# Sharing the last multiplication of a decoder step between VectorE and GpSimd

## The chip, the cores and the metric

The kernel runs on one core of a Trainium2 chip. The metric is device time in microseconds of one execution; the number compared is the median over several executions. Engine names: TensorE (PE) multiplies matrices into PSUM, VectorE (DVE) and ScalarE (ACT) work on PSUM and SBUF, GpSimd (POOL) is used here on SBUF only, SyncE (SP) issues DMAs. Stores of the result are issued from the queues of SyncE and ScalarE.

## What is computed

One decoding step of a hybrid layer for 256 prompt tokens and 32 sample tokens (288 columns, `NT`): RMSNorm, one wide input projection into a gated convolution, sparse attention and memory attention, one output projection, a residual addition and a last RMSNorm. Only that last norm is touched:

```python
def rms_norm(x, g):
    xf = x.astype(jnp.float32)
    y = xf * lax.rsqrt(jnp.mean(xf * xf, axis=-1, keepdims=True) + NORM_EPS)
    return (y * g.astype(jnp.float32)).astype(x.dtype)
...
    return x + mixed @ w_out, kv_new, win_state, conv_new
...
    y_prompt = rms_norm(xp, final_g)
    y_sample = rms_norm(xs, final_g)
```

## The kernel before

The model width of 2048 lies as 16 planes of 128 partitions, tokens along the free axis, so the result `ysum` is a tile of 128 x 16 x 288 floats in SBUF, and `o_y` in DRAM has the same layout. The schedule is written by hand: Python generators (`spawn`, `then`, `chunk`) place vector work between groups of matmuls, and each engine executes its instructions in the order in which the program issues them. Waits between engines are semaphores that the framework puts in.

The output projection runs in two passes over the 16 planes (`first_pass`, `second_pass`). In the second, each plane `n` leaves its product in PSUM, VectorE adds it to `ysum[:, n, :]`, ScalarE squares it for the sum over the width, and ScalarE multiplies the plane by the weight `final_g`. `first_pass` moves a plane from PSUM to SBUF with ScalarE (`act.activation(ysum[:, n, :], z, AF.Copy)`, 128x288).

After the last plane the tail runs in this order: the sums of squares (`ssq`, by matmuls with a column of ones), `rsqrt` on ScalarE and VectorE (a column of 1/rms per token group), `spread_tokens`, six small matmuls that spread these over all partitions into the PSUM tile `rb` (128 x 288), and then the loop over `OUT_PIECES`. This loop multiplies pieces of 1, 2, 2, 3, 3, 3 and 2 planes of `ysum` in place by `rb` on VectorE, and issues one store per piece, in turn on ScalarE's queue (even pieces) and SyncE's (odd pieces).

GpSimd has run nothing but DMA issues for a while then; earlier in the kernel it multiplies one half of each pair of pages of the compressed cache by weights (`cmp_use`, line 341, 128x512), beside VectorE, which takes the other half. Names of the tail in the profile: `ysum<-ysum,rb` are the multiplications, `o_y<-ysum` the stores (line 1443). Vector and scalar instructions go through a helper and show line 134.

Of the kernel before, what the change touches and what calls it, by code (L numbers as in the profile page):

```python
# [12 lines left out]
AF = mybir.ActivationFunctionType  # L13
ALU = mybir.AluOpType
# [8 lines left out]
NT = NTP + NTS  # L23
# [46 lines left out]
WARM = 5  # L70
LOW_FIRST = 22
TAIL_BUSY = (5, 7)
OUT_PIECES = (1, 2, 2, 3, 3, 3, 2)


@with_exitstack
def decode_step(ctx, tc, xT, xN, memT, cst, w_in, w_mem, w_out, w_bg, pt, ptv, ckc, ckk, ckv, wk, wv, mk, mv,
                o_y, o_kv, o_mem, o_conv, o_wk, o_wv):
    nc = tc.nc
# [29 lines left out]
    def matmul(out, a, b, **kw):  # L109
        n = size(out)  # L110
        k, t = ((0, n / 2400 + 0.0115) if b.dtype == F32R else (1, n * 0.00048 + 0.008) if out.shape[0] == 32
                else (2, max(0.21, n * 0.00143)))
        if k != kind[0]:
            at[0] += 0.2 if 1 in (k, kind[0]) else 0.08
        kind[0] = k
        at[0] += t
        nc.tensor.matmul(out, a, b, **kw)  # L117
# [19 lines left out]
    vec, act = Timed(nc.vector, VEC, 0.03, 0.0011), Timed(nc.scalar, ACT, 0.16, 0.00083)  # L137
# [44 lines left out]
    def zt(tag, name=None):  # L182
        return pzt.tile([128, NT], F32, name=name or tag, tag=tag)
# [682 lines left out]
    def spread_tokens(out, r, groups):  # L866
        for i, (_, c0) in enumerate(groups):
            n = 128 - c0
            matmul(out[:, i * 128:i * 128 + n], r[:, i:i + 1].to_broadcast([128, 128]), ident[:, c0:], start=True, stop=True)
# [513 lines left out]
    def busy(n):  # L1383

        for _ in range(n):
            matmul(rb[:, :NT], y2[:, 0, 0:128], y2[:, 0, :], start=True, stop=True)

    acc = zt("C", "yacc")
    rb = pss.tile([128, 512], F32, name="rb", tag="s")
# [46 lines left out]
    rsqrt(r, ssq[:, 0:3])  # L1436
    busy(TAIL_BUSY[1])
    spread_tokens(rb, r, GROUPS)
    n = 0
    for i, m in enumerate(OUT_PIECES):  # L1440
        yv = ysum[:, n:n + m, :]
        vec.tensor_tensor(yv, yv, rb[:, :NT].unsqueeze(1).to_broadcast([128, m, NT]), op=ALU.mult)
        (nc.sync if i % 2 else nc.scalar).dma_start(o_y[:, n:n + m, :], yv)
        n += m

# [118 lines left out]
```

## Time and profile before

| | us |
|---|---|
| three runs | 623.99, 628.30, 629.73 |
| their median | 628.3 |
| profiled execution, own time | 625.25 |
| its span (first to last instruction) | 622.8 |

The profile comes from one execution. Its page gives the busy time of each engine and the costliest groups of instructions; the trace behind it can be asked for a stretch of time, for the instructions of one tile, or for the chain of waits. Times of rows are microseconds from the start of the span unless they are marked ns. A group row gives the instruction with its shapes, its count, its busy time in us and the mean ns of one.

### The profile page before, as it was taken

The numbers are of one execution on the slowest core, as the hardware profiler recorded it, in microseconds if no ns is written. First come the engines' busy times: TensorE is split into PE (matmuls) and PEld (weight loads), VectorE is DVE, ScalarE is ACT, GpSimd is POOL, SyncE is SP. The second block draws the span as 40 slices with busy tenths as digits, with TensorE's granted clock in tenths as the row PEclk, the third lists the DMA queues.
The fourth block names the chain that finished last, engine by engine and source line by source line (L and its number), as shares of the span: only waits on it lengthen the run. The fifth ranks groups of instructions, "written<-read, shape, count | busy, mean of one in ns | idle before, by whom it ended". The sixth has DMA issues, their size and how long they took to land.

```text
span 622.8 us, 13340 instructions
## 1 busy us (share of the span) xinstructions
PE 604.3 (97%) x4895; PEld 558.4 (90%) x4895; DVE 458.2 (74%) x735; ACT 287.2 (46%) x500; POOL 209.4 (34%) x288
## 2 busy tenths in 40 slices
PE   8999999999999999999999999999999999999993
PEld 6889999989999799988988888889889889999993
DVE  3779899979587489978976879959586543457764
ACT  4665445454555334334434444434534444346560
POOL 1122654534236234324454532323112444122200
PEclk9999999999999999999999999999999999999997
DMA  8999799989989998978888798989979999478823
GB/s 267 367 412 405 272 334 307 337 303 350 322 270 359 375 356 292 383 294 280 281 328 274 247 373 277 314 302 302 382 271 327 338 313 323 140 244 299 233 95 152
DMA packets 74627, 188.40 MB, mean 302 GB/s; under 512 B 8945, under 2 KB 25842, under 8 KB 74178
## 3 DMA queue, kind: packets, MB, share of 16 engines
q0 software_dynamic: 27232, 105.10, 48.3%
q1 hardware_dynamic: 46320, 81.17, 37.1%
q10 hardware_dynamic: 1010, 1.28, 0.6%
q8 instruction: 38, 0.62, 0.4%
q14 instruction: 27, 0.22, 0.1%
HBM read 182.31 MB, written 13.60 MB: 315 GB/s over the span
## 4 chain that ended last, share of the span: by engine, by line
PE 83%; DMA 10%; DVE 3%; ACT 1%; issue 1%; SPq 1%; ACTq 0%; DVEq 0%
PE z L117 67%; DMA st<-ckk 4%; PE od L117 3%; DMA st<-xN 2%; PE sk L117 2%; PE acc L117 2%; PE s L117 1%; DMA mraw<-memT 1%; DMA st<-ckc 1%; DMA qk<-ckk 1%; PE pv L122 1%; DVE ysum L134 1%; DMA rows_v<-ptv 1%; PE pt L122 1%; PE omd L117 1%
## 5 line engine op out<-in xcount | busy, mean ns | idle before, releaser
L117 PE MATMUL z<-x,wh 128*128 128x288 f32 x1664 | 255.1, 302 | 0.4 <-ACT wh L134 0.4
L134 DVE TENSOR_TENSOR wl<-w,wh 128x1024 fp32r<-128x1024 f32 x148 | 184.5, 1247 | 80.6 <-PE z L117 45.1
L117 PEld LDWEIGHTS z<-x,wh 128*128 128x128 f32 x1664 | 229.9, 188 | 9.5 <-issue 7.3
L134 ACT ACTIVATE wh<-w 128x1024 fp32r<-128x1024 f32 x148 | 155.0, 1052 | 22.3 <-PE z L117 20.5
L117 PE MATMUL z<-x,wl 128*128 128x288 f32 x832 | 127.0, 295 | 0.2 <-DVE wl L134 0.2
L117 PEld LDWEIGHTS z<-x,wl 128*128 128x128 f32 x832 | 115.7, 188 | 0.4 <-DVE wl L134 0.4
L341 POOL TENSOR_TENSOR st<-st,cst 128x512 f32<-128x512 f32 x56 | 64.8, 1160 | 117.5 <-issue 55.4
L218 POOL DMA_DIRECT2D w<-w_in x104 | 58.1, 559 | 95.0 <-DVE wl L134 77.3
L134 DVE TENSOR_REDUCE pooled<-st 128x16 f32<-128x1024 f32 x56 | 67.8, 1211 | 10.1 <-POOL st L341 10.1
L134 DVE TENSOR_TENSOR st<-st,cst 128x512 f32<-128x512 f32 x56 | 40.0, 716 | 2.6 <-DMA st<-ckc 2.5
L563 POOL DMA_INDIRECT st<-ckv,rows_v x29 | 31.5, 1087 | 26.8 <-PE od L117 13.9
L218 POOL DMA_DIRECT2D w<-w_out x32 | 17.5, 551 | 58.6 <-DVE wl L134 44.8
L117 PE MATMUL z<-y,wh 128*128 128x288 f32 x256 | 37.0, 297 | 0.0
L117 PE MATMUL z<-y1a,wh 128*128 128x288 f32 x224 | 35.2, 298 | 0.0
L117 PEld LDWEIGHTS z<-y,wh 128*128 128x128 f32 x256 | 35.1, 188 | 0.0
L117 PEld LDWEIGHTS z<-y1a,wh 128*128 128x128 f32 x224 | 31.5, 188 | 1.6 <-issue 0.8
L117 PE MATMUL z<-m,wh 128*128 128x256 f32 x192 | 27.1, 286 | 1.8 <-ACT wh L134 1.8
L117 PEld LDWEIGHTS z<-m,wh 128*128 128x128 f32 x192 | 24.5, 190 | 2.8 <-ACT wh L134 2.2
L134 ACT ACTIVATE P<-P,nm 128x128 f32<-128x128 f32 (+1 forms) x32 | 14.2, 445 | 26.5 <-DVE nm L134 26.5
L117 PE MATMUL sk<-st,qz 128*32 128x256 f32 x288 | 21.6, 382 | 2.2 <-DMA st<-ckk 2.2
L134 ACT ACTIVATE ysum<-z 128x288 f32<-128x288 f32 x16 | 6.6, 412 | 34.1 <-PE z L117 34.1
L117 PE MATMUL z<-y,wl 128*128 128x288 f32 x128 | 19.6, 295 | 0.0
(274 smaller groups left out, 703.0 us busy)
## 6 DMA issues: line engine op xcount, KB each, us to landing
w<-w_in POOLq DMA_DIRECT2D x104, 512.0 KB
st<-ckc SPq DMA_DIRECT2D x112, 256.0 KB
w<-w_out POOLq DMA_DIRECT2D x32, 512.0 KB
st<-ckk SPq DMA_DIRECT2D x112, 128.0 KB
w<-w_mem POOLq DMA_DIRECT2D x11, 512.0 KB
o_wk<-wk POOLq DMA_DIRECT2D x8, 512.0 KB
o_wv<-wv POOLq DMA_DIRECT2D x8, 512.0 KB
qk<-ckc SPq DMA_DIRECT2D x16, 256.0 KB
```

The source lines that it names most:

```text
L117: nc.tensor.matmul(out, a, b, **kw)
L122: nc.tensor.transpose(out, a, b)
L134: return getattr(self.engine, name)(*args, **kw)
L218: (nc.gpsimd if s >= WR else nc.sync).dma_start(raws[s], wsrc[s])
L341: done.append(eng.tensor_tensor(tm[:, :, kv], tm[:, :, kv], acmp[:, kv].unsqueeze(1).unsqueeze(1).to_broadcast([128, 2, 4, 64]), op=ALU.mu ...
L563: nc.gpsimd.indirect_dma_start(t, None, ckv, bass.IndirectOffsetOnAxis(ap=rows_v[:, j * 4 + b:j * 4 + b + 1], axis=0))
```

## The change

VectorE no longer multiplies all 16 planes. Each entry of `OUT_PIECES` is now a pair (engine, planes): VectorE takes pieces of 1, 2, 2, 3, 2 and 1 planes (eleven), GpSimd pieces of 2, 2 and 1 (five). GpSimd's pieces use a copy of the factors in SBUF, `rs`, that ScalarE makes from `rb`; VectorE goes on reading `rb` in PSUM. There are nine stores instead of seven, still in turn on ScalarE's queue and SyncE's.

```diff
-OUT_PIECES = (1, 2, 2, 3, 3, 3, 2)
+
+OUT_PIECES = ((0, 1), (0, 2), (1, 2), (0, 2), (0, 3), (1, 2), (0, 2), (1, 1), (0, 1))
...
     spread_tokens(rb, r, GROUPS)
+    rs = zt("A", "rbs")
+    act.activation(rs, rb[:, :NT], AF.Copy)
     n = 0
-    for i, m in enumerate(OUT_PIECES):
+    for i, (e, m) in enumerate(OUT_PIECES):
         yv = ysum[:, n:n + m, :]
-        vec.tensor_tensor(yv, yv, rb[:, :NT].unsqueeze(1).to_broadcast([128, m, NT]), op=ALU.mult)
+        (nc.gpsimd if e else nc.vector).tensor_tensor(yv, yv, (rs if e else rb[:, :NT]).unsqueeze(1).to_broadcast([128, m, NT]),
+                                                      op=ALU.mult)
         (nc.sync if i % 2 else nc.scalar).dma_start(o_y[:, n:n + m, :], yv)
         n += m
```

## Rows read from the trace of the kernel before

**Rows 1.** The page: an engine's busy time, share, instructions; one costly group of VectorE.

```profile
PE 604.3 (97%) x4895; PEld 558.4 (90%) x4895; DVE 458.2 (74%) x735; ACT 287.2 (46%) x500; POOL 209.4 (34%) x288
...
L134 DVE TENSOR_TENSOR st<-st,cst 128x512 f32<-128x512 f32 x56 | 40.0, 716 | 2.6 <-DMA st<-ckc 2.5
```

**Rows 2.** Chain of waits, 600 us to the end: shares, then start, us, what.

```profile
by line: PE z L117 38.6%; DVE ysum L134 22.4%; PE ssqy L117 7.0%; PE rb L117 3.8%; DVEq L1560 2.9%; DVE yt L134 1.5%; ACT ysq L134 1.4%; issue 1.2%; ACT yr L134 1.2%; DVE yr L134 1.2%; DVE yv L134 0.7%
...
613.46 0.45 DVE ysum L134
...
614.58 4.22 DVE ysum L134 x5
```

**Rows 3.** Windows of the tail: busy us per engine; last PEclk, DMA share, GB/s.

```profile
614.75:615.20 0.45, 0.00 (x0) 0.00 (x0) 0.45 (x2) 0.00 (x0) 0.00 (x0) 1.00 0.83 297
...
616.90:617.10 0.20, 0.00 (x0) 0.00 (x0) 0.20 (x2) 0.00 (x0) 0.00 (x0) 0.50 0.31 104
617.10:621.10 4.00, 0.00 (x0) 0.00 (x0) 1.70 (x3) 0.00 (x0) 0.00 (x0) 0.50 1.01 404
621.10:622.80 1.70, 0.00 (x0) 0.00 (x0) 0.00 (x0) 0.00 (x0) 0.00 (x0) 0.50 0.01 4
...
618.00:618.50 0.50, 0.00 (x0) 0.00 (x0) 0.50 (x2) 0.00 (x0) 0.00 (x0) 0.50 1.08 436
```

**Rows 4.** The DMA view from 614 us to the end: packets, bytes.

```profile
DMA packets 1008, 2.36 MB, mean 262 GB/s; under 512 B 112, under 2 KB 240, under 8 KB 1008
```

**Rows 5.** Timeline of the tail: start us, us, engine, operation; a row can merge several.

```profile
613.95 0.35 ACTq L1443 DMA_DIRECT2D o_y<-ysum  x1
...
613.84 1.41 DVE L134 TENSOR_TENSOR ysum<-ysum,rb 128x576 f32<-128x576 f32 x2
...
614.50 1.71 DVE L134 TENSOR_TENSOR ysum<-ysum,rb 128x576 f32<-128x576 f32 x2
614.64 0.34 SPq L1443 DMA_DIRECT2D o_y<-ysum  x1
...
616.28 0.34 SPq L1443 DMA_DIRECT2D o_y<-ysum  x1
...
618.88 0.34 ACTq L1443 DMA_DIRECT2D o_y<-ysum  x1
```

**Rows 6.** Groups of VectorE by form: count, busy us, mean ns of one.

```profile
L134 DVE TENSOR_TENSOR P<-s,cst 128x512 f32<-128x512 f32 x12 | 8.2, 686 | 1.2 <-PE s L117 1.1
...
L134 DVE TENSOR_TENSOR ysum<-ysum,rb 128x864 f32<-128x864 f32 x3 | 3.0, 1048 | 0.0
...
L134 DVE TENSOR_TENSOR ysum<-ysum,rb 128x576 f32<-128x576 f32 x3 | 2.2, 747 | 0.0
...
L134 DVE TENSOR_TENSOR ysum<-ysum,rb 128x288 f32<-128x288 f32 x1 | 0.5, 453 | 0.9 <-PE rb L117 0.9
```

**Rows 7.** Instructions of the tile `ysum`: ns min/median/max, first and last start us.

```profile
L134 ACT ACTIVATE ysum<-z x16: 411/412/413, 500.1 to 557.6; 128x288 f32<-128x288 f32 x16
```

**Rows 8.** Instructions of line 341, GpSimd: ns min/median/max, first and last start.

```profile
L341 POOL TENSOR_TENSOR st<-st,cst x56: 1078/1083/2128, 64.3 to 431.3; 128x512 f32<-128x512 f32 x56
```

**Rows 9.** Timeline of VectorE and GpSimd side by side, three stretches.

```profile
64.29 1.23 DVE L134 TENSOR_TENSOR wl<-w,wh 128x1024 fp32r<-128x1024 f32 x1
64.34 2.13 POOL L341 TENSOR_TENSOR st<-st,cst 128x512 f32<-128x512 f32 x1 [0.18 <-DMA st<-ckc]
65.43 1.58 DVE L134 TENSOR_TENSOR st<-st,cst 128x512 f32<-128x512 f32 x1
...
322.68 0.68 DVE L134 TENSOR_TENSOR qk<-qk,cst 128x512 f32<-128x512 f32 x1
323.28 0.68 DVE L134 TENSOR_TENSOR P<-s,cst 128x512 f32<-128x512 f32 x1
323.45 1.09 POOL L341 TENSOR_TENSOR qk<-qk,cst 128x512 f32<-128x512 f32 x1 [3.10 <-DVE qk L134]
...
431.32 1.08 POOL L341 TENSOR_TENSOR st<-st,cst 128x512 f32<-128x512 f32 x1 [4.62 <-DVE st L134]
```

## The prediction

> **What bounds the kernel now.** I read the page first, then the last microseconds, because the edit touches nothing before them. Over the whole span TensorE is busy 97% [rows 1]; the edited loop starts only after TensorE's last matmul, so the page's averages say nothing about it. The chain of waits from 600 us on puts 22.4% of those 22.8 us on VectorE's `ysum` operations, and its last two VectorE pieces (613.46 and 614.58) run to the end of the last instruction, 618.80 [rows 2]. Read alone, that says VectorE's seven multiplications set the end. But the chain follows instructions, and the span lasts 4.0 us longer than the last multiplication. What fills these 4 us stands in the windows: from 617.10 to 621.10 the DMA engines are busy all the time (share 1.01) at 404 GB/s, then 1.70 us pass in which nearly nothing moves, and the span ends [rows 3]. So the end is set by a transfer: the seven `o_y` pieces, 2.36 MB [rows 4], which leave as fast as 16 DMA engines take them.
>
> The windows also show where the engines are not full after the first packet at about 614.80: at 614.75 to 615.20 (297 GB/s, the single first plane), from there to 615.45 (nothing left to send), and once more at 616.90 to 617.10 (104 GB/s) [rows 3]. The last gap has a plain cause: the fourth piece was issued at 616.28 [rows 5], and its packets come about 0.82 us after the issue (the second piece: issued 614.64, packets from 615.45). From 617.10 on every piece is issued before the engines get to it. Only multiplications that come earlier than those gaps can move the end.
>
> **The change part by part.** VectorE before: seven pieces, from 613.46 to 618.80 [rows 2], 5.34 us. One plane takes 453 ns, two 747, three 1048 [rows 6]; in the timeline, where a row can merge pieces and its start is the first one's, the next piece starts 0.38 us after a single plane and 0.66 after two [rows 5], some 0.08 before the other's end, so 0.96 after three. After: pieces of 1, 2, 2, 3, 2 and 1 planes, starting at 613.46, 613.84, 614.50, 615.16, 616.12 and 616.78, ending at 613.91, 614.59, 615.25, 616.21, 616.87 and 617.24. VectorE is done 1.56 us earlier.
>
> ScalarE's copy of the factors, PSUM to SBUF, 128x288: the same form as `first_pass`, 412 ns [rows 7]. It waits for the same matmul as VectorE, so it runs from 613.46 to 613.87, beside VectorE's first piece, and is out of ScalarE's queue before the first store (613.95 in [rows 5]) is due. That the two read one PSUM tile together is not in the trace; if one had to wait for the other, it costs GpSimd's start 0.45 us at most, which below still changes nothing. Its buffer of tag A was last used for the convolution, which the output projection needs as input; the wait for it is free.
>
> GpSimd: two pieces of two planes and one of one plane. The trace has its two-operand operation with 512 elements only: median 1083 ns [rows 8]. Scaled with the elements, 576 take 1.22 us and 288 take 0.61. It starts 0.09 us after its releaser (VectorE's `qk` ends 323.36, GpSimd starts 323.45 [rows 9]), so at 613.96, and ends its pieces at 615.18, 616.40 and 617.01. The two engines finish within 0.25 us of each other.
>
> Stores: nine instead of seven; an issue takes 0.34 us on its queue and starts about 0.05 us after its piece [rows 5]. ScalarE's queue: 613.95, 615.23 (behind GpSimd's first piece), 616.26, 616.92, 617.29. SyncE's: 614.64, 615.30, 616.45 (behind GpSimd's second), 617.06. Queued behind GpSimd's first piece are three stores of VectorE; none is ready before it. The last issue moves from 618.88 to 617.29, 1.59 us.
>
> The drain: the first two stores (one plane, two planes, VectorE, 613.95 and 614.64) are what they were, so packets again start at 614.80, with the same pause, and flow from 615.45. Left then are 2.36 - 0.147 = 2.21 MB. The store of 615.23 brings packets at 616.05, before the 0.295 MB of the second piece are out (615.45 + 0.295/0.404 = 616.18); those of 615.23 and 615.30 last until 617.64, and the next packets come from 617.08. No pause is left. At 404 GB/s the 2.21 MB take 5.47 us, to 620.92; before it was 621.10. With the same 1.70 us behind it the span ends at 622.6 instead of 622.8. **The sum is -0.18 us:** the whole of what 1.56 us of VectorE buys is the pause at 616.90.
>
> Bounds. Two more one-plane pieces than before: if each moves at the first plane's 297 GB/s instead of 404, each costs 0.13 us, and the sum becomes +0.08. If the rate rises above 404 GB/s, the nearest higher row is a half microsecond at 436 [rows 3]; 2.21 MB at it give 620.52, -0.58. I take -0.2, since the pause is certain to go and 297 GB/s includes the ramp of the first packet. Then -0.2 is 625.05 against the profiled execution's own 625.25, and 628.1 against the median 628.3 of the runs shown.
>
> **A rule against it.** VectorE and GpSimd disturb each other in this trace. At 64.29 VectorE subtracts `wl<-w,wh`, both in SBUF; GpSimd's multiplication, started at 64.34, takes 2.13 us instead of 1.08, and VectorE's next, `st<-st,cst`, 1.58 instead of 0.72 [rows 1, 8, 9]. At 323.28 VectorE runs `P<-s,cst`, one operand in PSUM, 0.68 us, its mean over twelve, and GpSimd beside it 1.09 [rows 6, 9]: no effect. In the changed loop VectorE keeps `rb` in PSUM, so I price the overlap at nothing. The Trainium skill, "SBUF — State Buffer", section "Who interferes with whom", says that a VectorE instruction with two SBUF inputs contends with a GpSimd instruction that reads SBUF and that one with a single SBUF input does not; both rows agree.
>
> **The rivals.**
> A: *the drain follows the last issue.* Then the end moves by the 1.59 us: 626.7. For it speaks the chain [rows 2]; against it 4.00 us of full engines [rows 3], of which no multiplication is part. 0.04.
> B, slower: *the two engines take turns after all.* Place: VectorE's second piece. GpSimd begins when that ends, at 614.6, and from there each piece waits for the other engine's: GpSimd's end at 615.8, 617.7 and 619.3, VectorE's at 616.5, 618.7, 620.0 and 620.4. The stores follow in this order, their packets 0.82 us behind the issue; the three-plane piece's come at 619.57, and from there 1.03 MB are left, 2.55 us, to 622.1: +1.0 us, 629.3. It decides as soon as GpSimd's first piece ends over 1.04 us after 615.18: the stores of 614.64 and 615.30 feed the engines until 616.91, 0.86 us past 616.05, and 0.18 is the gain to be used up. For it: the pair at 64.34; against it: the pair at 323.45 [rows 9]. 0.08.
> C: *GpSimd's first multiplication starts late,* having run none since 431.32 [rows 9]. Every microsecond past 1.04 is one on the end, since its own store and three of VectorE's leave ScalarE's queue in order. The trace's worst operation is 1.05 us longer than its median [rows 8], which would end where the kernel before does, at 628.3; its first, at 64.34, shows nothing beyond the overlap above. 0.04. The Trainium skill, "GPSIMD Engine Reference", section "Instruction dispatch", gives about 6 us for the first call of a freshly loaded kernel. By that the end would be an estimated 4.9 us later, 633.2; no row here shows such a load.
>
> **How the numbers follow.** The forecast has 0.84, A 0.04, B 0.08, C 0.04. Each lies within 1%, about what a measurement of this kernel can tell from no change, and the four times priced from rows, 626.7 to 629.3, within half of that. What is left is scatter: the three runs shown lie from 623.99 to 629.73, wider than all rivals together. So within 1% 0.95, faster 0.02, slower 0.03. The likeliest one's own range by the bounds is 627.7 to 628.4 on the median; since a median of a few new runs may fall anywhere in that scatter, the range is the lowest run less 0.2 and the highest plus 0.4 (less than half of B): 623.8 to 630.1.
>
> **What would show it.** VectorE's `ysum<-ysum,rb` group six times, 453, 747 and 1048 ns as before, over at about 617.2; three GpSimd multiplications of about 1.2, 1.2 and 0.6 us, the first at 613.96; a last issue near 617.3; DMA engines full from 615.45 to 620.9 without the pause; 1.7 us after it. Wrong: VectorE pieces longer than those forms (B), a GpSimd start after 615.0 (C), a drain that ends with the last issue, near 619.5 (A), or any difference before 613.4, where the edit has nothing.

## The result and the profile after

| | before | after |
|---|---|---|
| median of all runs, us (number of runs) | 624.83 (22) | 628.77 (22) |
| lowest to highest | 622.08 to 629.82 | 626.81 to 631.79 |
| profiled execution, own time | 625.25 | 626.81 |
| its span | 622.8 | 625.1 |

The ratio is 1.0062 with a 95% interval of 1.0045 to 1.0079. The changed kernel is slower by about 3.9 us; the forecast had it 0.2 us faster. That 628.1 stands close to 628.77 is an accident: the forecast was built on 628.3, the median of the three runs known then, and 22 runs of the kernel before give 624.83.

The two profiled executions differ upstream of the edit too: the last six matmuls into `rb` end at 613.44 before and at 611.45 after, 0.02 before the instruction that reads `rb` first. From the chain of waits (start us, us), before and after:

```profile
612.57 0.87 PE rb L117 x6
```

```profile
610.58 0.87 PE rb L118 x6
```

I compare tails from there: before, the span ends 622.8 - 613.44 = 9.36 us later; after, 625.1 - 611.45 = 13.65. The tail has grown by 4.29 us, and that is the loss of the median (3.94) within its scatter. All times "in the tail" below count from the end of these six matmuls. Spans are read to 0.1 us, so the difference of two tails is good to about 0.1.

The page of the kernel after, its line of busy times, is as blind to this as that of before [rows 1]: GpSimd is busy 3.9 us more, in three more instructions.

```profile
span 625.1 us, 13347 instructions
...
PE 605.1 (97%) x4895; PEld 559.8 (90%) x4895; DVE 456.8 (73%) x734; ACT 287.3 (46%) x501; POOL 213.3 (34%) x291
```

The timeline of the kernel after, from 611 us (start us, us, engine, operation; a row merges several; in brackets the idle time before it and who ended it):

```profile
611.47 0.41 ACT L135 ACTIVATE rbs<-rb 128x288 f32<-128x288 f32 x1 [1.81 <-PE rb L118]
611.91 3.77 DVE L1445 TENSOR_TENSOR ysum<-ysum,rb 128x288 f32<-128x288 f32 x6 [1.39 <-ACT rbs L135]
611.96 3.52 POOL L1445 TENSOR_TENSOR ysum<-ysum,rbs 128x576 f32<-128x576 f32 x3 [22.90 <-ACT rbs L135]
612.40 4.60 ACTq L1447 DMA_DIRECT2D o_y<-ysum  x5
613.09 2.75 SPq L1447 DMA_DIRECT2D o_y<-ysum  x4
```

VectorE is done in 3.77 us instead of 5.34, as forecast. But it starts only when ScalarE's copy is over: 0.46 us after the matmuls, where before it started after 0.02. Its pieces keep their lengths beside GpSimd (groups of VectorE and GpSimd by form, count, busy us, mean ns of one; against 453, 747 and 1048 in [rows 6]); GpSimd's are longer than forecast:

```profile
L1445 POOL TENSOR_TENSOR ysum<-ysum,rbs 128x576 f32<-128x576 f32 x2 | 2.8, 1399 | 22.9 <-ACT rbs L135 22.9
...
L1445 DVE TENSOR_TENSOR ysum<-ysum,rb 128x576 f32<-128x576 f32 x3 | 2.2, 745 | 0.0
L1445 DVE TENSOR_TENSOR ysum<-ysum,rb 128x864 f32<-128x864 f32 x1 | 1.0, 1044 | 0.0
...
L1445 POOL TENSOR_TENSOR ysum<-ysum,rbs 128x288 f32<-128x288 f32 x1 | 0.8, 785 | 0.0
```

None of this is 4 us long. The windows of the kernel after (columns as in [rows 3]) show where they are: the stores fill the DMA engines as forecast, stop before 620, and then 5.1 us pass in which no engine computes and nothing moves. Before, 1.70 us lay behind the stores.

```profile
617.00:618.00 1.00, 0.00 (x0) 0.00 (x0) 0.00 (x0) 0.00 (x0) 0.00 (x0) 0.50 1.03 402
618.00:619.00 1.00, 0.00 (x0) 0.00 (x0) 0.00 (x0) 0.00 (x0) 0.00 (x0) 0.50 1.03 383
619.00:620.00 1.00, 0.00 (x0) 0.00 (x0) 0.00 (x0) 0.00 (x0) 0.00 (x0) 0.50 0.53 184
620.00:621.00 1.00, 0.00 (x0) 0.00 (x0) 0.00 (x0) 0.00 (x0) 0.00 (x0) 0.50 0.00 0
621.00:625.10 4.10, 0.00 (x0) 0.00 (x0) 0.00 (x0) 0.00 (x0) 0.00 (x0) 0.50 0.00 0
```

What runs in those 5.1 us is not counted as work of an engine. It stands among the instructions that end the program, all under one line number (L1564 after, L1560 before): each engine drains, meets the others at semaphores and stops. The rows give count, ns min/median/max, first and last start. The kernel after:

```profile
L1564 POOLq EVENT_SEMAPHORE  x4: 17/17/17, 624.3 to 624.9; - x4
L1564 POOLq DRAIN  x3: 51/103/12309, 611.9 to 624.8; - x3
L1564 SPq DRAIN  x3: 7/7/7, 620.4 to 624.5; - x3
```

The kernel before:

```profile
L1560 POOLq EVENT_SEMAPHORE  x4: 17/17/17, 622.1 to 622.7; - x4
L1560 POOLq DRAIN  x3: 51/103/10903, 590.4 to 622.6; - x3
L1560 SPq DRAIN  x3: 7/7/7, 622.0 to 622.3; - x3
```

GpSimd has a drain that lasts 10.9 us even before the change. There it starts at 590.4, beside GpSimd's last DMA issue, and ends at 601.3, more than 20 us ahead of the end and under TensorE's last matmuls: nobody waits for it. After the change three multiplications at the very end stand ahead of it. It starts at 611.9 (GpSimd's sequencer gets there while the multiplications run) and ends at 611.92 + 12.31 = 624.23, that is 8.75 us after the last multiplication's end (615.48). SyncE, which waits for the stores, is through at 620.4 and then waits for GpSimd until 624.3. Before, SyncE came last: at 622.0, and GpSimd's semaphore followed at 622.1.

The waits of SyncE (waited for: us in total, times, longest) show the length of this, under a wrong name. After, from 605 us on:

```profile
SPq L1564 <- PEq L1564: 4.5, 2, 4.0
```

Before:

```profile
SPq L1560 <- PEq L1560: 0.7, 2, 0.5
```

TensorE's sequencer is named, but it had drained at once (its drains end within 1 us of 610.6 and of 624.6). SyncE waits for several engines here, and the one that came last was GpSimd. The chain of waits is no help either: after as before it ends with VectorE's multiplications (615.69) and shows nothing behind them.

The Trainium skill, "PSUM — Partial Sum Buffer", section "Engine vs sequencer instructions", says that a drain waits until its engine is fully idle. The trace agrees that it outlasts the multiplications behind which it stands. Why it lasts 8.75 us beyond them is what the experiments are about.

### The profile page after: what moved, and what is told of

Its sections match the earlier page's. It is cut to its first block, busy times and chain, and to the rows that moved or that the text cites. A ratio compares the mean times of both kernels' runs of the same rounds, so it can differ in the third digit from the quotient of the medians.

```text
span 625.1 us, 13347 instructions
## 1 busy us (share of the span) xinstructions
PE 605.1 (97%) x4895; PEld 559.8 (90%) x4895; DVE 456.8 (73%) x734; ACT 287.3 (46%) x501; POOL 213.3 (34%) x291
## 4 chain that ended last, share of the span: by engine, by line
PE 87%; DMA 5%; DVE 4%; issue 1%; ACT 1%; DVEq 0%; SPq 0%; ACTq 0%
PE z L118 68%; PE od L118 3%; DMA st<-ckk 3%; PE sk L118 3%; PE zf L118 2%; PE acc L118 2%; PE s L118 2%; DVE pooled L135 2%; DMA w<-w_mem 1%; PE pt L123 1%; PE pv L123 1%; DMA cst<-cst 1%; DVE wl L135 1%; DVE st L135 1%; PE omd L118 1%
## 5 line engine op out<-in xcount | busy, mean ns | idle before, releaser
L135 ACT ACTIVATE se<-z 128x288 f32<-128x288 f32 x16 | 6.5, 409 | 28.7 <-PE z L118 28.7
```

Of the source, the lines that this page charges most:

```text
L135: return getattr(self.engine, name)(*args, **kw)
```

## The experiments

Two causes were to be separated, besides the nine stores themselves (S in the expectations): the drain of GpSimd, and VectorE's wait for ScalarE's copy (W). For the drain there were two theories: it clears up behind the DMAs that GpSimd issued, and does so once (D1), or the late multiplications ahead of it make it long, whatever GpSimd did before (D2).

**e1: GpSimd drained early.** The kernel after, with a drain of GpSimd put behind its last DMA issue, while TensorE still works.

```diff
+    nc.gpsimd.drain()
     r = small(3, "yr")
     rsqrt(r, ssq[:, 0:3])
```

> The changed kernel with one explicit drain of GpSimd put into its queue after its last store issue and before the tail (it can run some 20 us before the tail, while GpSimd has nothing to do); the framework's own drain at the end stays. Tail here means: from the end of the six rb matmuls to the end of the span, 9.4 us before the change and 13.7 after it. Theory D1 (the end waits for GpSimd's last drain, and what is long in it is clearing up behind the DMAs that GpSimd issued, once): the explicit drain takes about 10 us unseen, the last one well under 1 us, the tail is 9.5 to 10 us, and the time is that of the kernel before within 0.5 us plus or minus. Theory D2 (the last drain is long because of the multiplications that precede it): the last drain still ends about 8.8 us after GpSimd's last multiplication, the tail stays near 13.7 us, 4 us slower than before. Rival S (the nine stores or their landing set the end): no change from the changed kernel, 4 us slower, whatever the drain does.

Measured: 624.78 us (10 runs) against 624.89 of the kernel before (19 runs), ratio 0.9997, interval 0.9970 to 1.0024. The added drain (its own line, L1436) and the last ones, instructions by line:

```profile
L1436 POOLq DRAIN  x1: 11819/11819/11819, 588.6 to 588.6; - x1
...
L1565 POOLq DRAIN  x3: 39/103/3630, 612.1 to 621.1; - x3
L1565 SPq DRAIN  x3: 7/7/7, 620.5 to 620.8; - x3
```

The added one lasts 11.8 us, from 588.6 to 600.45, where nobody waits for it. The last then ends at 612.12 + 3.63 = 615.75, only 0.07 us after the last multiplication, and SyncE comes last again. The tail is 9.76 us instead of 13.65. So the 8.7 us are not the price of a late GpSimd instruction: they are left over from what GpSimd did earlier, can be cleared early, and 3.89 us of them were on the end. D2 falls by this, and S too, since the nine stores are those of the kernel after.

**e2: one late element.** The kernel before, with one multiplication of a single element on GpSimd after VectorE's last piece, its result used by nothing.

```diff
+    late = small(1, "late")
+    nc.gpsimd.tensor_tensor(late, ysum[:, 15, 0:1], ysum[:, 15, 1:2], op=ALU.mult)
```

> The kernel before, with VectorE's seven multiplications and seven stores as they were, plus one GpSimd multiplication of one element per partition that can only run after VectorE's last piece; nothing reads its result. D1 and D2: GpSimd's last drain ends 8 to 9 us after this operation, at some 5.4 + 0.2 + 8.8 us after the rb matmuls, so the tail is about 15 us instead of 9.4, 5 to 6 us slower than before, though no work was moved and no store added. Rival S: the stores are those of before, the tail stays 9.4 us, same time.

Measured: 631.3 us (4 runs), ratio 1.0106, interval 1.0044 to 1.0168. The timeline, then the drain among the instructions by line:

```profile
616.85 0.19 POOL L1446 TENSOR_TENSOR late<-ysum 128x1 f32<-128x1 f32 x1 [27.90 <-DVE ysum L134]
```

```profile
L1562 POOLq DRAIN  x3: 51/103/8976, 616.8 to 626.3; - x3
```

An instruction of 0.19 us puts the drain's end at 616.81 + 8.98 = 625.79, 8.75 us after its own end; the tail is 15.27, 5.91 more than before. The amount of work on GpSimd does not matter, only when its last instruction ends.

**e3: no copy, a factor that is there from the start.** The kernel after; GpSimd's five planes are multiplied by a constant table in SBUF instead of the factors, so these five planes are not normalized, and they can run as soon as each plane is there, before the tail.

```diff
-    rs = zt("A", "rbs")
-    act.activation(rs, rb[:, :NT], AF.Copy)
+    rs = C("cos")
```

> The changed kernel without ScalarE's copy; GpSimd multiplies its five planes by a table that lies in SBUF from the start instead of the factors (so that these five planes of the output are not normalized), and so doesn't wait for rb: its planes are ready before the last plane is. Same eleven planes on VectorE, same nine stores. D1 and D2: GpSimd is through with its multiplications by about 4 us before the loop starts on VectorE, its drain ends 8.8 us later, before the stores have landed, so the tail is 9.4 less 0.2 to 1 us, as the transfers alone give it, and the time is that of before or up to 1 us faster. Rival S: nine stores as in the changed kernel, so the tail stays near 13 us and it is some 4 us slower.

Measured: 624.59 us (10 runs), ratio 0.9978, interval 0.9945 to 1.0011. Timeline, then the drain:

```profile
615.96 3.77 DVE L1444 TENSOR_TENSOR ysum<-ysum,rb 128x288 f32<-128x288 f32 x6 [0.95 <-PE rb L118]
```

```profile
L1563 POOLq DRAIN  x3: 51/103/9486, 609.7 to 624.8; - x3
```

Without the copy VectorE starts 0.02 us after the matmuls again. GpSimd's last piece ends at 610.41, the drain again 8.75 us behind it, at 619.16, still ahead of the stores. The tail is 9.16 us, 0.20 less than before. Within the reading that is the -0.18 that the forecast worked out for the transfers, with neither of the two costs it lacked.

**e4: the copy alone.** The kernel before, with ScalarE's copy added and used by nothing.

```diff
+    rs = zt("A", "rbs")
+    act.activation(rs, rb[:, :NT], AF.Copy)
     n = 0
     for i, m in enumerate(OUT_PIECES):
```

> The kernel before plus ScalarE's copy of rb to SBUF alone, which nothing reads; VectorE keeps all sixteen planes in seven pieces, no work on GpSimd. Theory W (VectorE has to wait until ScalarE has read the same PSUM tile): VectorE's first piece starts 0.45 us after the rb matmuls instead of 0.02, every store 0.44 us later, and the tail from the end of those matmuls to the end of the span is 9.8 us instead of 9.4. Rival (the wait seen in the changed kernel came from GpSimd's part): VectorE starts at once, tail 9.4 us.

One run, 624.22 us; the tail is what is read here, 9.81 us, 0.45 more than before. The timeline:

```profile
612.51 0.41 ACT L134 ACTIVATE rbs<-rb 128x288 f32<-128x288 f32 x1 [1.81 <-PE rb L117]
612.95 5.34 DVE L134 TENSOR_TENSOR ysum<-ysum,rb 128x288 f32<-128x288 f32 x7 [1.39 <-ACT rbs L134]
```

Both engines only read `rb`, and yet VectorE waits for the copy's end and 0.03 us more. The Trainium skill, "PSUM — Partial Sum Buffer", section "PSUM bank collisions raise a hardware error", says that ScalarE and VectorE must not access one bank of PSUM (in the same partitions) at the same moment, reads included, and that software has to keep them apart. The trace agrees: a semaphore from ScalarE to VectorE is there, and it costs 0.45 us.

**e5: one piece on GpSimd.** The kernel after, with GpSimd's share cut from three pieces to one, the third.

```diff
-OUT_PIECES = ((0, 1), (0, 2), (1, 2), (0, 2), (0, 3), (1, 2), (0, 2), (1, 1), (0, 1))
+OUT_PIECES = ((0, 1), (0, 2), (1, 2), (0, 3), (0, 3), (0, 3), (0, 2))
```

> The changed kernel with only the first GpSimd piece left (two planes); VectorE takes the other fourteen in pieces of 1, 2, 3, 3, 3 and 2, seven stores. D1 and D2: GpSimd's last multiplication ends 2.1 us earlier after the rb matmuls (1.9 us instead of 4.0), its last drain ends 2.1 us earlier, and the tail is about 11.6 us. Rival S: seven stores as before, and VectorE's last piece about 1 us later than in the changed kernel: the tail is about 9.8 us, before plus the wait of VectorE for the copy.

One run, 628.06 us; the tail is 11.5. The drain:

```profile
L1564 POOLq DRAIN  x3: 51/103/10201, 615.2 to 625.9; - x3
```

It ends at 625.37, 8.76 us after the single piece (616.61). With e2, e3 and after, this makes four places of the last multiplication and one distance, 8.75 to 8.76 us.

**e6: the copy from a bank of its own.** e1, with the factors spread a second time into another PSUM tile, from which ScalarE copies.

```diff
     spread_tokens(rb, r, GROUPS)
+    rb2 = pz.tile([128, 512], F32, name="rb2", tag="z")
+    spread_tokens(rb2, r, GROUPS)
     rs = zt("A", "rbs")
-    act.activation(rs, rb[:, :NT], AF.Copy)
+    act.activation(rs, rb2[:, :NT], AF.Copy)
```

> The changed kernel with the early drain of GpSimd, and with the factors spread a second time into a PSUM tile of their own (six more small matmuls), from which ScalarE copies. W and D1 together: VectorE's first piece starts within 0.1 us of the first six matmuls' end, GpSimd about 0.9 us later than in the changed kernel, and the tail from the end of the first six matmuls is 9.2 to 9.4 us, 0.2 us or less shorter than before the change: the time of before within what can be measured. If W is wrong: VectorE still starts 0.4 us late, tail 9.8 us.

Measured: 624.1 us (10 runs) against 624.54 (13 runs), ratio 0.9996, interval 0.9969 to 1.0023. The timeline:

```profile
613.51 3.78 DVE L1448 TENSOR_TENSOR ysum<-ysum,rb 128x288 f32<-128x288 f32 x6 [0.95 <-PE rb L118]
614.18 0.41 ACT L135 ACTIVATE rbs<-rb 128x288 f32<-128x288 f32 x1 [2.48 <-PE rb L118]
...
614.67 3.52 POOL L1448 TENSOR_TENSOR ysum<-ysum,rbs 128x576 f32<-128x576 f32 x3 [23.57 <-ACT rbs L135]
```

VectorE no longer waits. But the copy comes 0.67 us later, behind six more matmuls, and GpSimd's pieces with it; the tail is 9.4, the one of before. What is saved on VectorE's side may go on GpSimd's, whose last piece now ends 0.9 us after VectorE's; no run separates this.

**e7 to e10: what the drain clears.** The kernel after, with the early drain placed ahead of one of the 16 window copies that GpSimd issues along the kernel, so that 1, 20, 69 or 141 of GpSimd's 213 DMA issues come behind it (`n == 15`, `8`, `6`, `3`).

```diff
+                    if n == 15:
+                        nc.gpsimd.drain()
                     nc.gpsimd.dma_start(out, in_)
```

> The changed kernel with the explicit drain one store earlier: GpSimd issues one more store (the last of the window) after it, where the early drain left none. Theory P (the last drain clears up for every DMA that GpSimd issued since the drain before, 213 of them in the changed kernel, at about 0.04 us each): it ends within 0.5 us of GpSimd's last multiplication, tail 9.8 us as with the early drain. Theory F (one DMA since the last drain is enough for the whole price): it ends 8.8 us after it, tail 13.7 us as in the changed kernel.

> The changed kernel with the explicit drain some 45 us earlier, at the ninth of the sixteen window stores, so that GpSimd issues 20 DMAs after it. The drain stands before weight loads there, so the time before the tail may grow by some microseconds. P: the last drain ends about 0.8 us after GpSimd's last multiplication, the stores set the end, tail 9.8 us. F: 8.8 us after it, tail 13.7 us. A length between these, with e7 short: the price follows something else that the DMAs leave, up to a limit.

> The changed kernel with the explicit drain at the seventh window store, so that GpSimd issues 69 DMAs after it. So far the last drain outlasted GpSimd's last multiplication by 0.07 us with no DMA behind the drain before, 0.16 with one, 1.71 with 20 and 8.76 with all 213. If the price grows by 0.08 us with each DMA up to a limit: 69 give 5.5 to 6 us, and the last drain ends after the stores by a little (tail 10.5 us). If it follows the time passed or a share of all DMAs (69 of 213): about 2.8 us, hidden behind the stores, tail 9.8 us.

> The changed kernel with the explicit drain at the fourth window store, so that GpSimd issues 141 DMAs after it. With 0.08 us for each DMA up to a limit: 8.7 us, as with all 213, tail 13.6 us. With a share of all DMAs: 5.8 us, tail 10.8 us.

One run each: 626.69, 622.56, 624.83 and 626.29 us. The added drains of e8, e9 and e10:

```profile
L685 POOLq DRAIN  x1: 7654/7654/7654, 546.5 to 546.5; - x1
```

```profile
L685 POOLq DRAIN  x1: 6777/6777/6777, 419.5 to 419.5; - x1
```

```profile
L685 POOLq DRAIN  x1: 7780/7780/7780, 217.6 to 217.6; - x1
```

The last drains of e7 to e10, in this order:

```profile
L1566 POOLq DRAIN  x3: 51/103/3712, 615.6 to 624.6; - x3
```

```profile
L1566 POOLq DRAIN  x3: 51/103/5272, 610.8 to 619.8; - x3
```

```profile
L1566 POOLq DRAIN  x3: 51/103/9277, 612.7 to 622.5; - x3
```

```profile
L1566 POOLq DRAIN  x3: 51/103/6176, 615.2 to 624.2; - x3
```

| DMA issues of GpSimd since its previous drain | end of the last drain after the last multiplication, us | tail, us |
|---|---|---|
| 0 (e1) | 0.07 | 9.76 |
| 1 (e7) | 0.16 | 9.74 |
| 20 (e8) | 1.71 | 9.75 |
| 69 (e9) | 5.72 | 10.56 |
| 141 (e10) | 2.62 | 9.74 |
| 213 (after) | 8.75 | 13.65 |

Up to 69 it grows by about 0.082 us with each DMA that GpSimd has issued ((5.72 - 0.07) / 69 = 0.082; e8: 1.64 / 20 = 0.082), twice the 0.04 that the expectations of e7 and e8 worked with. So it is GpSimd's DMA issues that are cleared, not its earlier multiplications. The time since the drain before fits worse: from e8 to e9 it grows 3.0 times (64 and 193 us), the price 3.45 times, and the issues 3.45 times.

But 141 issues cost less than 69: both expectations for e10, 8.7 and 5.8, missed. Something seems to clear most of them in between, without a drain in the program. By 0.082 the 2.62 us are worth 31 issues and the 8.75 us 106; these are the counts less 110 and 107, so that a reset after about that many would fit them. That is arithmetic on two points, and no run shows where it would happen. The added drains, behind 72 issues (e10), 144 (e9) and 193 (e8) since the start, do not grow with the count either: 7.8, 6.8 and 7.7 us. But GpSimd's last DMAs were still under way when they began, as they were not at the last drains, so these lengths cannot be set beside the table. What exactly is cleared, and when, stays open.

**e11: the price of GpSimd's pieces.** The kernel after; a one-element multiplication reads the copy, so that GpSimd starts when it did, and then the five planes are multiplied by e3's constant table (and so are not normalized).

```diff
     act.activation(rs, rb[:, :NT], AF.Copy)
+    late = small(1, "late")
+    nc.gpsimd.tensor_tensor(late, rs[:, 0:1], rs[:, 1:2], op=ALU.mult)
+    rs = C("cos")
```

> The changed kernel in which GpSimd first multiplies one element of ScalarE's copy (so that it starts when it did) and then its five planes by a table in SBUF in place of the factors (these planes of the output are not normalized). In the changed kernel two planes take GpSimd 1.40 us, beside VectorE at its own pieces; with the table, before VectorE's loop, they took 1.22. If VectorE's running beside it is what slows GpSimd: 1.40 us again. If it is the operand that ScalarE has just written: 1.22 us. The end is set by the last drain either way, as in the changed kernel, some 0.2 to 0.6 us apart.

One run, 626.61 us. Timeline, then GpSimd by form:

```profile
611.38 3.77 DVE L1448 TENSOR_TENSOR ysum<-ysum,rb 128x288 f32<-128x288 f32 x6 [1.39 <-ACT rbs L135]
...
611.58 3.01 POOL L1448 TENSOR_TENSOR ysum<-ysum,cst 128x576 f32<-128x576 f32 x3
```

```profile
L1448 POOL TENSOR_TENSOR ysum<-ysum,cst 128x576 f32<-128x576 f32 x2 | 2.4, 1192 | 0.0
```

Beside the same six pieces of VectorE, GpSimd takes 1.19 us with the table and 1.40 with the copy. So it is not VectorE's running beside it that lengthens the pieces. e6 agrees: there GpSimd's last piece runs from 617.40 on, behind VectorE's last (617.29), and takes 0.79 us as in the kernel after. The factor's tile makes the difference, and why it does stays open. (The 1.22 us that the expectation takes from e3 is one of two such pieces there; the other took 2.05.) The drain is again 8.75 us behind the last piece.

**Where the 4.29 us went.** 3.89 are GpSimd's last drain (13.65 less 9.76). The other 0.40 is what is left in e1, which has all of the change but the long drain at the end; it is about VectorE's wait for the copy (0.45 in e4), and the 0.05 between them is less than the tails can be read to. e1 and e6 bring the time back to that of the kernel before; no run was measurably faster than it.

## Why the prediction failed, step by step

**What bounds the kernel.** Right as far as it went: in the kernel before, the stores set the end. e3 moves it by -0.20, near the -0.18 that the step on the drain of the stores forecast, although VectorE is done 1.57 us earlier.

**The step that failed** is the sentence "With the same 1.70 us behind it the span ends". What lay behind the last store was taken over from [rows 3] as a constant. It is the meeting of all engines at the end of the program, and the last to come sets it. Before, that was SyncE, with the stores; GpSimd had been there since 601.3. The change gives GpSimd its last work at the end, and with it moves the drain, which lasts 8.75 us behind that work: to 12.78 us in the tail (624.23 - 611.45), where the stores let SyncE through at about 9.0 (620.4). The difference, 3.8, is the drain's share of the loss. The trace of before held the row, a GpSimd drain of 10.9 us that starts at 590.4; I read the groups of instructions, the chain and the windows, which leave it out, and did not ask what each engine executes last.

**The copy** "beside VectorE's first piece": wrong. I had seen that the order of two readers of one PSUM tile is not in the trace, bounded it at 0.45 us, and laid it on GpSimd. The size was right and the engine wrong: ScalarE, whose copy stands first in the program, reads first, VectorE waits, and there it is on the path, since everything behind it starts later (e4, +0.45).

**GpSimd's multiplications:** 1.40, 1.40 and 0.79 us instead of 1.22, 1.22 and 0.61, 3.52 instead of 3.05 in all. The scaled row was right for a table that lies in SBUF (e11, 1.19), not for the fresh copy. Whether this costs anything at the end no run separates.

**VectorE's pieces** were right to within 10 ns, also beside GpSimd, and the stores' rate too: 383 to 414 GB/s in the whole windows from 614 to 619.

**The rivals.** A fell: the last issue starts at 615.81, and the stores go on to 619.6. B fell: no piece of VectorE is longer, and GpSimd's end 3.5 us after their start. C named the right engine at the wrong end: GpSimd's first multiplication starts 0.08 us after the copy, and it is behind the last that the time is lost. The estimated 4.9 us that the prediction worked out from the Trainium skill, "GPSIMD Engine Reference", section "Instruction dispatch", is near the loss by chance: no late start is there, neither here nor before e2's single element, and e1 gets the loss back with a drain.

**The chances.** The ratio of 1.0062 lies within 1%, where 0.95 was put, but its interval leaves no change out, and the forecast's own range on the median, 627.7 to 628.4 around a base of 628.3, is a gain or next to nothing. The range for the measured median, 623.8 to 630.1, holds 628.77 only because it was drawn over the scatter of three runs. None of the cases held a loss of 3.9 us for a reason read from rows.

## What to carry to other kernels

Before giving an idle engine work at the end of a kernel, look at what the end of the program asks of that engine, its drain above all: a long one that was hidden because the engine was long done comes due. If GpSimd issues DMAs and then has late work, drain it explicitly after the last of them, while others work (here 3.89 us for one line). And where a second engine is to read a PSUM tile that is on the path, count its read as time of the first, or give it a bank of its own.

## What the runs showed of the hardware

- GpSimd's drain at the end of the program lasted 8.75 to 8.76 us beyond its last instruction in five kernels (after, e2, e3, e5, e11), whether that was 188 ns or 1.4 us long, and 0.07 us when the DMA issues had been drained before (e1, e6). It depends on GpSimd's DMA issues since the last drain: 0.16, 1.71 and 5.72 us for 1, 20 and 69, but 2.62 for 141 (one run each).
- VectorE started 0.44 us late because ScalarE read the same PSUM tile, in after and in e4, and on time where ScalarE had another tile (e6).
- GpSimd multiplied 128x576 by a table in 1.19 us and by a tile that ScalarE had just written in 1.40; neither changed VectorE's pieces of that size (one operand in PSUM): 747 and 745 ns beside GpSimd, 747 in the kernel before.
